# A two-layer streaming encoder: memory norm from four pair loads, GLU and all key blocks as three fp32r products, and a new order for the first stage

## Chip, core and metric

One core of one Trainium2 chip. The metric is the device time of one execution, in microseconds (us), as the median of several runs. TensorE multiplies matrices into PSUM banks; VectorE and ScalarE work on SBUF and PSUM tiles; GpSimd works on SBUF tiles; SyncE (SP) issues nearly all DMA loads from one queue, in order.

## The reference

512 frames of 1024 features run through two layers, each followed by cross-attention into 256 memory tokens.

```
mem_n = rms_norm(mem, mem_norm_g)
# layer 0
z = rms_norm(x) @ w_in                  # u_a, gate_a, val_b, glu_b, gate_b
y   = S5 scan of u_a (32 groups, complex states) + d * u_a
z   = gelu(y);  out = z * sigmoid(z @ glu_w + glu_b)
y_a = out * silu(gate_a)
c   = causal conv, width 31, of val_b * sigmoid(glu_b)
y_b = silu(layer_norm(c)) * silu(gate_b)
x   = x + concat(y_a, y_b) @ w_out
# layer 1: chunked attention, 16 heads, gated
# after each layer, 4 heads:
q, g = rms_norm(x) @ w_qg;  k, v = mem_n @ w_kv
x    = x + (softmax(q k^T / 16) v * silu(g)) @ w_o
```

All tensors are f32, and the final norm follows.

## The kernel before

Activations are kept with features on partitions: eight tiles of 128 features by 512 frames. A product of two f32 matrices is made of three products in fp32r: each operand is split into a high part (a rounding cast, ScalarE) and a low part (a subtraction, on GpSimd or VectorE), and TensorE adds high*high, high*low and low*high in one PSUM bank. `weights` (L172) loads a weight block into one of three `raw` buffers, casts it into one of two `whi` buffers and writes the rest into one of three `wlo` buffers; `proj` (L195) runs the 24 matmuls of a block in the order of sixteen with the high weights, then eight with the low ones. A few products are native f32: `whole` (L181) loads a block and TensorE multiplies it as it is. These are the GLU's four blocks (L917 to L922) and the key blocks 0, 1 and 2 of layer 0 (`NATIVE`, L659); the profile shows a native matmul as two records.

The first stage, up to about 262 us, is one list of jobs, `PLAN` (L700), in order of emission: `u` S5 inputs, `z` and `c` the convolution's gate and value (projections), `g` the eight gate projections, `v` a fourth of a convolution block (two of its eight weight tiles, 320 KB each, in `cw` buffers, L809), `t` the S5 tables, `a` the preparation of a scan (L528), `b` the scan of one of four slices (L550: TensorE, then some 11 us of VectorE), `o` its output (L599: TensorE, then a way through DRAM that changes the layout), `m` and `n` the sums and the scale of the memory norm, `l` and `s` the mean and the scale of the LayerNorm. Behind the list stand the gelu of the four S5 outputs (`zs`), `mem_norm` (L626), the GLU, the LayerNorm's application and the key and value blocks in `KVORDER`; then the output projection (`residual`, L946).

Emission order is not yet the order on the engines. A planner takes the recorded instructions, with its own costs for each, and draws up an order per engine before the run: by priority, which is the order of emission except in `tc.high_priority()`, by when inputs should be ready, and by when a buffer of the tile's tag is free (a tag has `bufs` slots). Inside `T.ordered` or `pinned` the order of emission is kept. On the chip each engine then runs its list in order and waits where it must. So matmuls of a projection and of a convolution block alternate in the trace.

`mem_norm` scales the memory by a broadcast in PSUM (`bcast`, L212, tag `acc`, one bank that the mean of the LayerNorm and all row sums use too). It loads eight tiles of 128 KB through two `mt` buffers; in layer 0 it also keeps unsplit copies in `uu` for the native keys. In layer 1 it runs beside the five last blocks of the attention's output projection (L1372).

At the start `first_c` and `third` (L777 to L782) are three projections in the three `proj` banks; the row scale `rb0` is broadcast behind the third, and the next projection needs a bank that `z0` (L792) has read.

## Time and profile before

| | |
|---|---|
| median of 3 runs | 997.92 us (994.61 to 998.61) |
| the profiled execution | 994.67 us |
| its span, first to last instruction | 992.9 us |
| TensorE busy | 956.0 us, 96% |
| weight loads of TensorE | 817.4 us, 82% |
| VectorE, ScalarE, GpSimd busy | 57%, 47%, 45% |
| mean granted TensorE clock | 0.991 |

How to read it: a busy TensorE record ends where the last result leaves, so the pace of a run of matmuls is read from the start of one group to the start of the next. The idle time before an instruction is followed by what ended it.

### The profile page before, as it was taken

To read this page: it belongs to the slowest core of one execution; us is meant where nothing else is said; L and a number is where in the kernel's file an instruction comes from. 1 tells how busy PE (TensorE), PEld (TensorE's weight loads), DVE (VectorE), ACT (ScalarE), POOL (GpSimd) and SP (SyncE) were. 2 spreads that over 40 slices of the span, in tenths; PEclk is the share of its full clock that TensorE was granted. 3 is DMA by queue.
4 is the path that set the end of the run, shared out by engine and by line. 5 is a ranking of instruction groups with operands and counts; after the bars stand their busy time and mean duration, and the time that the engine had idled before them with its cause. 6 is when DMAs were issued, how large, how long until landed. Compare 5 with 4: busy or idle time off the path is not lost.

```text
span 992.9 us, 14232 instructions
## 1 busy us (share of the span) xinstructions
PE 956.0 (96%) x5336; PEld 817.4 (82%) x5336; DVE 565.7 (57%) x1260; ACT 469.2 (47%) x845; POOL 442.3 (45%) x245
## 2 busy tenths in 40 slices
PE   9999999989999999999999999999999999999996
PEld 7788889759888888888787887878878998888895
DVE  7975257874344333452668767787667313333476
ACT  6333445565443434444456655656535543434352
POOL 1022333049676334457444435344327983443241
PEclk9999999999999999999999999999999999999998
DMA  8365656347523222223122222222214453222153
GB/s 290 119 191 180 195 157 191 104 159 229 162 98 91 79 81 69 64 96 107 64 75 75 75 68 92 75 75 75 64 43 138 151 189 107 64 85 76 52 169 107
DMA packets 53621, 113.71 MB, mean 115 GB/s; under 512 B 13233, under 2 KB 24625, under 8 KB 53553
## 3 DMA queue, kind: packets, MB, share of 16 engines
q1 hardware_dynamic: 53408, 112.74, 35.5%
q8 instruction: 42, 0.69, 0.3%
q14 instruction: 27, 0.21, 0.1%
q10 hardware_dynamic: 144, 0.07, 0.0%
HBM read 106.50 MB, written 6.29 MB: 114 GB/s over the span
## 4 chain that ended last, share of the span: by engine, by line
PE 34%; DVE 9%; issue 3%; ACT 2%; DMA 1%; POOL 1%; POOLq 0%; ACTq 0%; DVEq 0%
PE ps_proj L81 27%; PE ps_att L81 2%; PE ps_tr L84 2%; PE ps_acc L81 2%; PE ps_tr L81 1%; DVE pe L162 1%; ACT whi L168 1%; DVE ps_att L1270 1%; DVE tz L162 1%; DVE o L153 1%; DVE h L157 1%; POOL wlo L153 1%; ACT pe L1257 1%; DVE s L1269 1%; DMA mt<-in_memT_dram 1%
## 5 line engine op out<-in xcount | busy, mean ns | idle before, releaser
L153 POOL TENSOR_TENSOR wlo<-raw,whi 128x1024 fp32r<-128x1024 f32 x130 | 317.7, 2448 | 411.1 <-ACT whi L168 366.0
L81 PE MATMUL ps_proj<-h,whi 128*128 128x512 f32 x1184 | 299.4, 397 | 2.4 <-DVE ang L153 2.4
L81 PEld LDWEIGHTS ps_proj<-h,whi 128*128 128x128 f32 x1184 | 217.5, 188 | 47.4 <-issue 5.1
L168 ACT CAST whi<-raw 128x1024 fp32r<-128x1024 f32 x148 | 155.1, 1049 | 191.3 <-PE ps_proj L81 91.8
L81 PE MATMUL ps_proj<-h,wlo 128*128 128x512 f32 x592 | 151.7, 394 | 0.0
L81 PE MATMUL ps_proj<-og,whi 128*128 128x512 f32 (+1 forms) x672 | 135.0, 348 | 0.5 <-DVE og L153 0.5
L81 PEld LDWEIGHTS ps_proj<-h,wlo 128*128 128x128 f32 x592 | 111.0, 189 | 22.7
L81 PEld LDWEIGHTS ps_proj<-og,whi 128*128 128x128 f32 x672 | 107.6, 188 | 17.9 <-DVE og L153 2.0
L81 PE MATMUL ps_proj<-og,wlo 128*128 128x512 f32 (+1 forms) x344 | 73.4, 348 | 0.1
L81 PEld LDWEIGHTS ps_proj<-og,wlo 128*128 128x128 f32 x344 | 56.1, 188 | 8.9 <-POOL wlo L153 0.4
L153 DVE TENSOR_TENSOR pt<-ps_tr,pt 128x512 fp32r<-128x512 f32 (+1 forms) x80 | 39.9, 526 | 32.4 <-ACT pt L168 32.3
L168 ACT CAST pt<-ps_tr 128x512 fp32r<-128x512 f32 (+1 forms) x80 | 34.3, 460 | 49.1 <-PE ps_tr L84 48.8
L162 DVE TENSOR_SCALAR pe<-pe,s 128x256 f32<-128x256 f32 (+3 forms) x96 | 51.2, 555 | 1.4
L1257 ACT ACTIVATE pe<-ps_att,s 128x128 f32<-128x128 f32 (+3 forms) x64 | 33.6, 526 | 36.4 <-DVE s L162 32.5
L153 DVE TENSOR_TENSOR z<-ps_proj,rb 128x512 f32<-128x512 f32 x32 | 22.0, 688 | 46.3 <-PE ps_proj L81 46.2
L153 POOL TENSOR_TENSOR sa<-sa,sq 128x512 f32<-128x512 f32 (+1 forms) x28 | 38.9, 1388 | 18.9 <-ACT sq L228 18.2
L153 DVE TENSOR_TENSOR x<-ps_proj,x 128x512 f32<-128x512 f32 (+1 forms) x38 | 22.9, 603 | 41.7 <-PE ps_proj L81 41.7
L153 DVE TENSOR_TENSOR kv<-ps_proj,kv 128x256 fp32r<-128x256 f32 (+1 forms) x24 | 12.2, 511 | 60.2 <-ACT kv L168 59.3
L157 DVE SCALAR_TENSOR_TENSOR h<-x,par,h 128x512 fp32r<-128x512 f32 x24 | 38.6, 1613 | 13.5 <-ACT h L247 13.5
L84 PE MATMUL ps_tr<-ident,pe 128*128 128x128 f32 x224 | 35.9, 279 | 9.5 <-DVE pe L162 5.0
L81 PEld LDWEIGHTS ps_proj<-x,cw 128*128 128x128 f32 x320 | 39.1, 191 | 5.1 <-DMA cw<-in_cw_dram 3.1
L84 PEld LDWEIGHTS ps_tr<-ident,pe 128*128 128x128 f32 x224 | 27.1, 142 | 18.7 <-DVE pe L162 6.7
(244 smaller groups left out, 1448.3 us busy)
## 6 DMA issues: line engine op xcount, KB each, us to landing
raw<-in_xa_qg_dram SPq DMA_DIRECT2D x32, 512.0 KB, 3.4
...
```

Source lines behind the costliest of these rows:

```text
L81: return self.keep(nc.tensor.matmul(*args, **kw))
L84: return self.keep(nc.tensor.transpose(*args))
L153: (eng or V).tensor_tensor(out, a, b, op=op)
L157: V.scalar_tensor_tensor(out=out, in0=a, scalar=s, in1=b, op0=op0, op1=op1)
L162: V.tensor_scalar(out=out, in0=in0, scalar1=s1, scalar2=None, op0=op0)
L168: A.copy(hi, src)
L1257: A.activation(st_["pe"][i], ps[:, c:c + n], AF.Exp, bias=nb, accum_out=st_["sums"][:, i:i + 1])
L1269: V.reduce_max(init, ps[:, :nf], axis=AX.X)
L1270: V.tensor_tensor_reduce(out=ps[:, nf:n], in0=ps[:, nf:n], in1=st["tz"][:, MEM - (n - nf):], scale=1.0, scalar=init, op0=ALU.add, op1=ALU. ...
```

## The change

`mem_norm` takes four loads of two tiles each, all ahead of the broadcast, into `x` tiles in layer 0 and `kv` tiles in layer 1, and makes only the split form. The GLU's input is split, and its four blocks and all key blocks run as three products; `whole` is gone. Key and value weights of layer 0 have their low parts made on VectorE and GpSimd in turns (before: GpSimd), the GLU's on VectorE. Four key blocks come ahead of the LayerNorm's scale and of the GLU; `KVORDER` holds the rest. In `PLAN` `z0 c0` go ahead of `u0 u1`, `a1` ahead of `g2`, `b1` ahead of `z3 c3`, `a2` ahead of `g3`, `b2` ahead of `v2`, and `g4` to `g7` stand behind `b3`. The broadcast of `rb0` is put between the high and the low products of `third`. `cw` has three buffers instead of two, `s16` 28 instead of 48; the gated outputs are written over the gates.

```diff
--- before.py
+++ after.py
@@ -178,11 +178,6 @@
             split(raw, hi, lo, eng)
         return hi, lo
 
-    def whole(src, kt=8, n=P):
-        raw = tl("raw", (P, kt, n))
-        nc.sync.dma_start(raw, src)
-        return raw
-
     def mm3(ps, terms, cuts=()):
         prods = []
         for lo, hi in zip((0,) + tuple(cuts), tuple(cuts) + (len(terms),)):
@@ -256,7 +251,7 @@
             xs.append(t)
         return xs
 
-    l0p = Phase("l0", {"gate": 8, "uu": 8, "ev": 4, "cw": 2}).open()
+    l0p = Phase("l0", {"gate": 8, "uu": 8, "ev": 4, "cw": 3}).open()
 
     def norm_split(gname, goff=0):
         st = Stats()
@@ -623,28 +618,24 @@
             st.add(t, pin=True)
         return st
 
-    def mem_norm(rs, tag, raw_tag=None):
-        mm, raw = [], []
+    def mem_norm(rs, tag, load_tag):
+        mm = []
         with tc.high_priority():
+            ts_ = []
+            for i in range(0, KT, 2):
+                t = tl(load_tag, (P, 2, MEM))
+                nc.sync.dma_start(t, memT_d[i:i + 2].rearrange("i p s -> p i s"))
+                ts_ += [t[:, 0], t[:, 1]]
             rbm = bcast(rs, MEM)
-            for i in range(KT):
-                t = tl("mt", (P, MEM))
-                nc.sync.dma_start(t, memT_d[i])
+            for i, t in enumerate(ts_):
                 tt(t, rbm, t, ALU.mult)
                 e = rl(tag, (P, 2, MEM))
-                if raw_tag is None:
-                    mm.append(gsplit(t, pc("mem_g", i), e[:, 0], e[:, 1]))
-                else:
-                    if i % 2 == 0:
-                        m = tl(raw_tag, (P, 2, MEM))
-                    raw.append(m[:, i % 2])
-                    A.activation(raw[i], t, AF.Copy, scale=pc("mem_g", i))
-                    mm.append(split(raw[i], e[:, 0], e[:, 1], V))
-        return mm, raw
-
-    def token_major(outs, act, ws_d, eng=None):
+                mm.append(gsplit(t, pc("mem_g", i), e[:, 0], e[:, 1]))
+        return mm
+
+    def token_major(outs, act, ws_d, eng):
         for e in range(2):
-            wh, wl = weights(ws_d[e], kt=4, n=MEM, eng=eng)
+            wh, wl = weights(ws_d[e], kt=4, n=MEM, eng=eng())
             for low in range(2):
                 for t, o in enumerate(outs):
                     ts_ = slice(t * P, (t + 1) * P)
@@ -654,15 +645,15 @@
                             T.matmul(o, a[:, ts_], b[:, k, :], start=(e == 0 and low == 0 and t % 2 == 0 and k == 0 and j == 0),
                                      stop=(e == 1 and low == 1 and t % 2 == 1 and k == 3))
 
-    def kv_units(layer, mm, raw=None, native=()):
+    def kv_units(layer, mm, engs=(None,)):
+        count = [0]
+
+        def eng():
+            count[0] += 1
+            return engs[count[0] % len(engs)]
+
         def keys(i):
-            if ("k", i) in native:
-                w = whole(xa_k_d[layer, i])
-                ps = psum("proj")
-                for j in range(KT):
-                    T.matmul(ps[:, :MEM], w[:, j, :], raw[j], start=(j == 0), stop=(j == KT - 1))
-            else:
-                ps = proj(weights(xa_k_d[layer, i]), mm, n=MEM)
+            ps = proj(weights(xa_k_d[layer, i], eng=eng()), mm, n=MEM)
             e = rl("kv", (P, 2, MEM))
             with tc.high_priority():
                 split(ps[:, :MEM], e[:, 0], e[:, 1], V)
@@ -671,15 +662,7 @@
         def values(h):
             hi, lo = rl("kv", (P, 2, MEM)), rl("kv", (P, 2, MEM))
             ps = psum("proj")
-            if ("v", h) in native:
-                for e in range(2):
-                    w = whole(xa_v_d[layer, h, e], kt=4, n=MEM)
-                    for t in range(2):
-                        for j in range(4):
-                            T.matmul(ps[:, t * MEM:(t + 1) * MEM], raw[4 * e + j][:, t * P:(t + 1) * P], w[:, j, :],
-                                     start=(e == 0 and t == 0 and j == 0), stop=(e == 1 and t == 1 and j == 3))
-            else:
-                token_major([ps[:, :MEM], ps[:, MEM:]], mm, [xa_v_d[layer, h, e] for e in range(2)])
+            token_major([ps[:, :MEM], ps[:, MEM:]], mm, [xa_v_d[layer, h, e] for e in range(2)], eng)
             with tc.high_priority():
                 split(ps.rearrange("p (m c) -> p m c", m=2), hi, lo, V)
             vv[h] = (hi, lo)
@@ -695,12 +678,11 @@
             run["v"](i)
         return kv
 
-    KVORDER = [('k', 2), ('k', 0), ('k', 1), ('v', 3), ('k', 4), ('v', 0), ('k', 6), ('k', 3), ('k', 5), ('v', 2), ('v', 1), ('k', 7)]
-    NATIVE = [('k', 0), ('k', 1), ('k', 2)]
-    PLAN = "u0 u1 z0 c0 u2 u3 z1 c1 g0 v0 t0 g1 v0 v0 v0 a0 z2 b0 c2 v1 v1 v1 v1 g2 o0 a1 z3 b1 c3 v2 v2 v2 v2 g3 o1 a2 m0 g4 b2 v3 v3 v3 v3 g5 o2 a3 b3 n0 g6 l0 s0 o3 g7"
+    KVORDER = [('k', 4), ('v', 0), ('k', 5), ('v', 1), ('k', 6), ('v', 2), ('k', 7), ('v', 3)]
+    PLAN = "z0 c0 u0 u1 u2 u3 z1 c1 g0 v0 t0 g1 v0 v0 v0 a0 z2 b0 c2 v1 v1 v1 v1 a1 g2 o0 b1 z3 c3 a2 g3 o1 b2 v2 v2 v2 v2 a3 m0 v3 v3 v3 v3 o2 b3 g4 n0 g5 l0 g6 o3 g7"
     UENG = 'VVVVVVVVVVGG'
     GATE_V = (0, 3, 5, 7)
-    s5p = Phase("s5", {"l1": 2, "cs": 2, "m": 6, "g": 2, "y": 2, "s16": 48, "s32": 4}, side="right").open()
+    s5p = Phase("s5", {"l1": 2, "cs": 2, "m": 6, "g": 2, "y": 2, "s16": 28, "s32": 4}, side="right").open()
     l0cm = tc.tile_pool(name="l0s", bufs=1, side="right", reuse_waits="tile")
     l0 = l0cm.__enter__()
 
@@ -777,9 +759,14 @@
     first_c = [proj(weights(w_in_d[n], eng=V), h0) for n in (12, 8)]
     with tc.high_priority():
         rs0 = st0.done()
-    third = proj(weights(w_in_d[2], eng=V), h0)
-    with tc.high_priority():
-        rb0 = rb_tile(rs0)
+    third = psum("proj")
+    wh, wl = weights(w_in_d[2], eng=V)
+    for i, (a, b) in enumerate([(wh, 0), (wh, 1), (wl, 0)]):
+        for k in range(KT):
+            T.matmul(third, a[:, k, :], h0[k][b], start=(i == 0 and k == 0), stop=(i == 2 and k == KT - 1))
+        if i == 1:
+            with tc.high_priority():
+                rb0 = rb_tile(rs0)
     T.ordered = False
     tb = {}
 
@@ -886,11 +873,11 @@
             stt(conv[i], mu, -1.0 / 512, conv[i], ALU.mult, ALU.add)
             lst.add(conv[i], V)
 
-    def ln_scale(_):
+    def ln_scale():
         lst.rs = lst.done(1.0 / 512)
 
     stages = {"u": state_input, "z": conv_gate, "c": conv_input, "a": prep, "b": scan, "o": out, "g": gate, "m": mem_sums, "n": mem_scale, "v": conv_taps,
-              "l": ln_centre, "s": ln_scale, "t": tables}
+              "t": tables, "l": ln_centre}
     for job in PLAN.split():
         stages[job[0]](int(job[1:]))
     mrs = mem["rs"]
@@ -900,7 +887,7 @@
         t = tl("uu")
         stt(t, uP[sl].rearrange("p s j -> p (s j)"), pc("s5_d", sl), ys[sl].rearrange("p s j -> p (s j)"), ALU.mult, ALU.add)
         A.activation(t, t, AF.Gelu_apprx_tanh)
-        zs.append(t)
+        zs.append((t, split(t, rl("ev"), rl("uu"), V)))
 
     l0cm.__exit__(None, None, None)
     s5p.close()
@@ -909,33 +896,33 @@
     for i in range(8):
         if gates[i] is None:
             gate(i)
-    mm, mraw = mem_norm(mrs, "og", "uu")
+    mm = mem_norm(mrs, "og", "x")
+    run, kv0 = kv_units(0, mm, (G, V))
+    for i in range(4):
+        run["k"](i)
+    ln_scale()
 
     for g in gates:
         A.activation(g, g, AF.Silu)
     yg = [None] * 8
     for i in range(4):
-        w = whole(glu_w_d[i], 4)
-        ps = psum("proj")
-        for k in range(4):
-            T.matmul(ps, w[:, k, :], zs[k], start=(k == 0), stop=(k == 3))
-        sg = tl("ev")
+        ps = proj(weights(glu_w_d[i], kt=4, eng=V), [z[1] for z in zs])
+        sg = tl("sq")
         A.activation(sg, ps, AF.Sigmoid, bias=pc("glu_b", i))
-        tt(sg, zs[i], sg, ALU.mult, G)
-        o = tl("ev")
+        tt(sg, zs[i][0], sg, ALU.mult, G)
+        o = gates[i]
         tt(o.rearrange("p (j s) -> p j s", s=4), sg.rearrange("p (s j) -> p j s", s=4),
-           gates[i].rearrange("p (j s) -> p j s", s=4), ALU.mult)
+           o.rearrange("p (j s) -> p j s", s=4), ALU.mult)
         yg[i] = split(o, rl("og"), rl("og"))
 
-    run, kv0 = kv_units(0, mm, mraw, NATIVE)
     def ln_apply():
         lb = bcast(lst.rs, SEQ)
         for i in range(4):
             t = tt(conv[i], lb, conv[i], ALU.mult)
             A.activation(t, t, AF.Silu, scale=pc("ln_g", i), bias=pc("ln_b", i))
-            o = tl("ev")
+            o = gates[4 + i]
             tt(o.rearrange("p (j s) -> p j s", s=CP), t.rearrange("p (s j) -> p j s", s=CP),
-               gates[4 + i].rearrange("p (j s) -> p j s", s=CP), ALU.mult)
+               o.rearrange("p (j s) -> p j s", s=CP), ALU.mult)
             yg[4 + i] = split(o, rl("og"), rl("og"), V)
 
     ln_apply()
@@ -1369,7 +1356,7 @@
 
     kvp = Phase("kv1", {"kv": 16}, side="right").open()
     xap = Phase("xa1", XA).open()
-    mm, _ = mem_norm(mrs, "q")
+    mm = mem_norm(mrs, "q", "kv")
     residual(od_out_d, og, first=PARTS)
     h, st = norm_split("xa_g", 8)
     kv1 = kv_proj(1, mm)
```

## Rows read from the trace of the kernel before

**Rows 1.** The page of the whole span: busy time of each engine with its share of the span and instructions; and, from the costliest groups, the cast of a weight block (line, engine, operation, output<-inputs, shapes, count | busy us, mean ns of one | idle before, releaser).

```profile
PE 956.0 (96%) x5336; PEld 817.4 (82%) x5336; DVE 565.7 (57%) x1260; ACT 469.2 (47%) x845; POOL 442.3 (45%) x245
...
L168 ACT CAST whi<-raw 128x1024 fp32r<-128x1024 f32 x148 | 155.1, 1049 | 191.3 <-PE ps_proj L81 91.8
```

**Rows 2.** Busy time of the engines in the stretch from 192 to 262 us, from the GLU to the first block of the output projection. Columns: stretch, its length, busy us and instructions of each engine, granted TensorE clock, DMA share, GB/s.

```profile
192.00:262.00 70.00, 64.99 (x409) 53.58 (x408) 37.11 (x58) 41.01 (x64) 47.10 (x22) 1.00 0.57 182
```

**Rows 3.** TensorE's timeline, 32 to 45 us. Columns: start in us, length in us, engine, line, operation, output<-inputs, how many; in brackets the idle time before it and what ended it.

```profile
31.99 3.93 PE L81 MATMUL ps_proj<-h,whi 128*128 128x512 f32 x16
35.76 1.98 PE L81 MATMUL ps_proj<-h,wlo 128*128 128x512 f32 x8
37.58 1.02 PE L81 MATMUL ps_acc<-dg,ones 128*128 128x512 f32 x2
40.96 3.92 PE L81 MATMUL ps_proj<-h,whi 128*128 128x512 f32 x16 [2.36 <-DVE ang L153]
```

**Rows 4.** VectorE's timeline, 34 to 41 us.

```profile
34.65 0.87 DVE L162 TENSOR_SCALAR dg<-ident,s 128x128 f32<-128x128 f32 x4
...
37.20 1.22 DVE L153 TENSOR_TENSOR wlo<-raw,whi 128x1024 fp32r<-128x1024 f32 x1
...
39.27 1.02 DVE L153 TENSOR_TENSOR uu<-ps_att,rb 128x512 f32<-128x512 f32 x1
40.14 0.68 DVE L153 TENSOR_TENSOR ev<-ps_proj,rb 128x512 f32<-128x512 f32 x1
```

**Rows 5.** TensorE's timeline, the two holes of the middle of the first stage.

```profile
101.12 1.32 PE L81 MATMUL ps_proj<-x,cw 128*128 128x64 f32 x10 [1.62 <-DMA cw<-in_cw_dram]
...
155.59 1.30 PE L81 MATMUL ps_proj<-x,cw 128*128 128x64 f32 x10 [0.66 <-DVE m L153]
```

**Rows 6.** TensorE's timeline, the first and the last weight tiles of the first convolution block (`v0`).

```profile
62.85 2.33 PE L81 MATMUL ps_proj<-x,cw 128*128 128x64 f32 x20
...
83.91 1.22 PE L81 MATMUL ps_proj<-x,cw 128*128 128x64 f32 x10
```

**Rows 7.** The view of the convolution weight tiles: time from issue to landing of their 32 loads.

```profile
DMA to landing us min/median/max: 2.6/3.6/6.0
```

**Rows 8.** TensorE's timeline, 188 to 272 us.

```profile
188.98 1.09 PE L81 MATMUL ps_acc<-sa,ones 128*128 128x512 f32 x2
...
192.43 5.31 PE L81 MATMUL ps_proj<-uu,raw 128*128 128x512 f32 x12
197.58 0.95 PE L81 MATMUL ps_acc<-ones,sa 128*128 128x1 f32 x8
...
199.33 0.59 PE L81 MATMUL ps_acc<-dg,ones 128*128 128x256 f32 x2
...
205.37 5.40 PE L81 MATMUL ps_proj<-uu,raw 128*128 128x512 f32 x16 [1.15 <-ACT og L168]
212.55 3.72 PE L81 MATMUL ps_proj<-uu,raw 128*128 128x256 f32 x16 [1.79 <-ACT uu L641]
...
216.97 5.34 PE L81 MATMUL ps_proj<-uu,raw 128*128 128x256 f32 x24
...
226.30 1.20 PE L81 MATMUL ps_proj<-wlo,og 128*128 128x256 f32 x8 [1.38 <-POOL wlo L153]
...
242.01 1.98 PE L81 MATMUL ps_proj<-og,whi 128*128 128x256 f32 x16
243.82 1.07 PE L81 MATMUL ps_proj<-og,wlo 128*128 128x256 f32 x8
...
268.44 2.00 PE L81 MATMUL ps_proj<-og,whi 128*128 128x512 f32 x8
270.27 1.07 PE L81 MATMUL ps_proj<-og,wlo 128*128 128x512 f32 x4
```

**Rows 9.** VectorE's groups by form, 199 to 240 us: the gating of the LayerNorm branch's four tiles and of the GLU's four, and the scaling of the memory tiles. Columns as in rows 1.

```profile
L153 DVE TENSOR_TENSOR ev<-x,gate 128x512 f32<-128x512 f32 x4 | 9.9, 2505 | 0.8 <-ACT x L935 0.8
...
L153 DVE TENSOR_TENSOR ev<-ev,gate 128x512 f32<-128x512 f32 x4 | 5.2, 1298 | 1.0 <-POOL ev L153 0.9
L153 DVE TENSOR_TENSOR mt<-ps_acc,mt 128x256 f32<-128x256 f32 x8 | 3.2, 422 | 1.8 <-DMA mt<-in_memT_dram 1.2 <-PE ps_acc L81 0.4
```

**Rows 10.** VectorE's timeline, first and last work of the fourth scan (`b3`).

```profile
174.84 0.69 DVE L153 TENSOR_TENSOR m<-ps_att,cs 128x512 f32<-128x512 f32 x1 [4.97 <-PE ps_att L81]
...
184.70 1.28 DVE L153 TENSOR_TENSOR hh<-m,m 128x508 f32<-128x508 f32 x2
```

**Rows 11.** ScalarE's timeline, the copy of the last S5 output and the last gelu.

```profile
188.76 0.59 ACT L610 COPY y<-ps_att 128x512 f32<-128x512 f32 x1 [0.72 <-PE ps_att L81]
...
197.58 0.63 ACT L902 ACTIVATE uu<-uu 128x512 f32<-128x512 f32 x1 [1.15 <-DVE uu L157]
```

**Rows 12.** TensorE's timeline, second layer's attention.

```profile
484.52 0.30 PE L81 MATMUL ps_att<-qk,qk 128*128 128x128 f32 x1 [1.71 <-ACT qk L1160]
...
486.44 3.48 PE L81 MATMUL ps_proj<-h,wlo 128*128 128x512 f32 x8
```

**Rows 13.** Busy time by stretch, just behind those rows. Columns as in rows 2; the granted clock is a share of 2.4 GHz.

```profile
487.00:488.00 1.00, 1.00 (x3) 0.73 (x3) 0.15 (x1) 1.00 (x4) 0.14 (x1) 0.50 0.00 0
```

**Rows 14.** TensorE's timeline, the start of the second layer's key blocks.

```profile
771.06 2.08 PE L81 MATMUL ps_proj<-q,whi 128*128 128x256 f32 x16
...
776.56 1.22 PE L81 MATMUL ps_proj<-q,wlo 128*128 128x256 f32 x8 [0.55 <-POOL wlo L153]
```

## Prediction

> **What bounds the kernel now.** I read the page's busy shares first: TensorE is busy 96% of the span [rows 1], so a change counts only by what it does to TensorE's own work or to one of the few holes in it. Second, TensorE's timeline, where the bracket at a line's end is a hole and what ended it. From 270 us on the change touches almost nothing that TensorE does; before that the holes are a wait behind the first norm [rows 3], one for convolution weights and one for the scan [rows 5], and three at the end of the first stage, between the gated linear unit (GLU) and the first value blocks [rows 8]. Third, in that last stretch, the other engines: none of ScalarE, VectorE and GpSimd is full [rows 2], so those holes come from the order of the work, not from a full engine.
>
> **Part 1, three products instead of one native product.** GLU: sixteen native products of 512 columns, each two records. Twelve records, six products, start at 192.43 and the next work at 197.58 [rows 8]: 0.858 us each, 13.7 us. In the three-product form eight matmuls of 512 columns take from 268.44 to 270.27 [rows 8], 0.229 us each; 48 take 11.0. Saved: 2.7 us. Keys: 24 records, twelve native products of 256 columns, take 5.34 us, 0.445 each; three blocks have 24 products, 10.7 us. A three-product block runs sixteen matmuls from 242.01 to 243.82 [rows 8], 0.113 each, 24 in 2.7; three blocks 8.1. Saved: 2.6 us. Together 5.3 us of work that TensorE has no longer. The price lies elsewhere. ScalarE gets casts for three more key blocks at 1.05 [rows 1], four half-size ones for the GLU and four of its input, some 8 us. Of the layer's sixteen key and value weights half go to VectorE at 1.22 [rows 4], 9.8 us, and with the GLU's four and its input some 15. I put both at nothing, as ScalarE is busy 41 and VectorE 37 of 70 us there [rows 2]; if the cover goes, it shows as a wait for a weight split, of which the largest there now is 1.38 us [rows 8].
>
> **Part 2, the first norm's broadcast inside the third projection.** Its diagonal is written by 35.52 [rows 4]. The broadcast matmul starts at 37.58, behind the third projection's eight low products; the change puts it behind the sixteen high ones, at 35.76 [rows 3], 1.8 us sooner, and the copy to `rb` with it. The plan also puts `z0` ahead of `u0`: `z0` reads the projection bank that TensorE waits for, and now stands behind `u0`'s 1.02 us on VectorE, at 40.14 [rows 4]. What is late next is the weight split on VectorE, which ends at 38.42 [rows 4]; `z0` would be done at about 39.1, and TensorE, finished with the third projection at 38.6 as now, waits 0.5 us instead of 2.36 [rows 3]. Gain 1.8, bounds 0 and 2.36; I take 1.7.
>
> **Part 3, three buffers for convolution weights.** One wait of 1.62 us ends with such a load [rows 5]. A third slot starts each load one tile earlier; I take 1.3, between 0 and 1.62. The 0.66 us before 155.59 [rows 5] ends with the scan; 0.4 for it, between 0 and 0.66. The smaller rings for the tables I put at nothing: their operations follow each other on VectorE, and the table is long done when the first scan needs it.
>
> **Part 4, the plan and the end of the first stage.** Three holes, 1.15, 1.79 and 1.38 us, 4.3 together [rows 8]. Why they are there: the memory's broadcast runs at 199.33, though the mean that occupies the same single bank was computed at 188.98; the normaliser's sums, which the program puts first, take the bank at 197.58 [rows 8]. So the eight memory tiles come late, and the key blocks meet them. In the change `ln_scale` goes behind four key blocks, so the broadcast follows the mean; and the four pair loads no longer wait for two small buffers to be read. Where do the scans go? The last scan holds VectorE from 174.84 to 185.98 [rows 10]. Behind it the old plan has `g6`, `o3`, `g7`; the new has `g4`, `g5`, `g6`, `o3`, `g7`, two projections of 24 times 0.229, 11.0 us, more. So the mean, which waits for that scan on VectorE, comes some 11 us sooner as TensorE counts, and the memory's broadcast with it: about 182 on the old clock, when TensorE reaches the keys at 192.4. Eight tiles at 0.42 for the scaling [rows 9] and, with GpSimd quiet, about as much for the low half need some 9 us: in time. The last output leaves TensorE at 188.76 and its gelu ends at 198.2 [rows 11], 9.5 us, and the new split adds 1.3; behind it now stand `g7`, 5.5 us, and four key blocks, 10.8. So the GLU finds its input ready. All 4.3 us could go; I leave 1.3 for key weights, which are split in turns on GpSimd and VectorE. Gain 3.0, from 4.3 to a loss worked out under the second rival.
>
> **Part 5, the second layer's memory norm.** Its loads move from `mt` into `kv` tiles, four instead of eight, ahead of five residual blocks on SP's queue. The keys start at 771.06 without a hole, right behind the residual [rows 14], so earlier memory tiles bring nothing. The 0.55 us before 776.56 ends with a weight split on GpSimd, which the change does not touch [rows 14]. If the new loads come late, VectorE, in order, stands with the last head's output behind it; the rows show no such wait, so I bound it by the longest hole of the early stage, 2.36, and by a gain of 0.55, and take 0.
>
> **Sum.** 5.3 + 1.7 + 1.3 + 0.4 + 3.0 = 11.7 us. The profiled execution took 994.67 us (span 992.9, 1.8 around it), so 983.0. It is the lower end of the runs shown; their median, 997.92, lies 3.25 above it, and I give the forecast on the median: 986.2 us.
>
> **Rivals.**
>
> First, *only the work goes*: the order on each engine is drawn up by a planner before the run, so what I say of the plan need not come out, and holes of the same size may open elsewhere, as they did at 101.12 and 155.59 [rows 5]. Then 5.3 us remain: 997.92 - 5.3 = 992.6. For it: the holes have different causes, so no one remedy takes them all. Against it: each has one in the change that I can follow. Chance 0.16.
>
> Second, *the memory tiles are late all the same*. VectorE's two-input operations here are slow beside a busy GpSimd: the gating of a tile took 1.30 us for the GLU's four and 2.51 us for the four behind them, when weight splits ran on GpSimd without a break [rows 9]. Every second key block has its weights split on GpSimd, just then. At 0.42 plus 2 us for a tile, eight need 19.4 us instead of 9; broadcast at 182, they end at 201.4, when the first key block should end at 195.1: TensorE stands some 6 us, and the new splits behind it on VectorE cost 2 or 3 more. Net gain 11.7 + 1.3 - 9 = 4.0: 993.9. The Trainium skill, page GPSIMD Engine Reference, section 8 (Key points), says that GpSimd shares its memory interfaces with VectorE and that operations with two inputs there contend. By that rule this rival would hold whenever GpSimd splits a block. The trace agrees on the slowing [rows 9]. Against it: with half the splits on VectorE, GpSimd is no longer busy without a break. Chance 0.12.
>
> Third, *slower: the convolution weights become the pace*. The new plan puts `v2` four times and `v3` four times with only `a3` and `m0` between: sixteen weight tiles. Each is about 1.1 us of TensorE (two in 2.33, with the last one's end); now eight of them are spread from 62.85 to 85.1 [rows 6], with projections between. Three slots give a tile every third of landing plus 1.1 us: 1.57 at the median landing of 3.6, 2.37 at the longest of 6.0 [rows 7]. Sixteen tiles then lack 7.5 to 20.3 us, unless the planner moves `g4` and `g5` in between. If it does not, the time is slower by half a per cent once more than 16.7 us are lost, at landings of 5.3 us and up; at 5.7 it is 18.7, giving 997.92 - 11.7 + 18.7 = 1004.9. It would be dearer still if TensorE's clock fell: after the hole of 1.71 us at 484.52 the clock was granted at 0.50, which is 1.2 GHz, and eight matmuls took 3.48 us [rows 12, 13] instead of 1.98 [rows 3]. The Trainium skill, page TensorE: Matmul & The Clock Gate, Part 1, says the same of an engine that has idled; behind the holes of the early stage it stayed at 1.00 [rows 2], so the sum has none. Against the rival: TensorE does interleave projections with these tiles now. Chance 0.08.
>
> Fourth, *everything goes*: 5.3 + 2.4 + 1.6 + 0.7 + 4.3 + 0.55 = 14.9 us: 983.1. Chance 0.1.
>
> **How the numbers follow.** The forecast, with its bounds on parts 2 to 5, covers 983.5 to 990 and has 0.54. The range takes in the fourth rival, counted from the profiled execution instead of the median (994.67 - 14.9 = 979.8), and the first two: 980 to 995. Outside are the third rival and tails of the rest, 0.16. About 0.5%, 5.0 us, is what a measurement here can tell from no change. Faster by more: forecast, fourth rival and half of the first (it lies on the edge), 0.72. Within: the other half and the second, 0.2. Slower: the third, 0.08.
>
> **What would show it.** Right: GLU and key blocks as runs of sixteen and eight; a hole of under 1 us in place of the one at 40.96; the memory's broadcast on TensorE ahead of the normaliser's sums; key blocks with no hole ahead of the GLU; the output projection starting some 11 us sooner. Wrong: a hole before the first key block ended by a memory tile (second rival), convolution tiles at 1.6 us and more apart with nothing between (third), holes of 4 to 6 us in new places (first). Were the sum right at the output projection and wrong at the end, the loss would lie in the second layer's memory norm or in the planner's order behind it.

## The result, and the profile after

The changed kernel takes 1011.54 us (median of four runs, 1008.03 to 1015.16), the kernel before beside it 997.79: ratio 1.015, 95% interval 1.0114 to 1.0185. The forecast was 986.2 us, 11.7 less than before; it is 13.75 more. The profiled execution took 1009.22 us.

First, the page: the span, and the busy time of the engines with share and instructions (answers to [rows 1]).

```profile
span 1007.4 us, 14325 instructions
PE 964.3 (96%) x5376; PEld 831.5 (83%) x5376; DVE 589.8 (59%) x1276; ACT 473.5 (47%) x848; POOL 433.3 (43%) x240
```

TensorE is busy for 8.3 us longer, though it has less to do. So the lost time is not only in holes: matmuls take longer.

Second, where. TensorE's timeline at the start of the output projection, which had begun at 261.59 (the kernel before) and has the same work behind it in both:

```profile
275.44 1.99 PE L81 MATMUL ps_proj<-og,whi 128*128 128x512 f32 x8
277.27 1.08 PE L81 MATMUL ps_proj<-og,wlo 128*128 128x512 f32 x4
```

13.85 us later. From there to the end it is 732.0 us here and 731.3 before: by these two profiles everything was lost in the first stage.

Third, TensorE's timeline there; the bracket is the idle time ahead of the line and what ended it. From 37 to 62 us (answers to [rows 3]):

```profile
37.83 3.94 PE L81 MATMUL ps_proj<-h,whi 128*128 128x512 f32 x16 [0.47 <-DVE ev L153]
...
51.51 5.51 PE L81 MATMUL ps_proj<-h,whi 128*128 128x512 f32 x16 [2.48 <-DVE uu L153]
56.86 2.01 PE L81 MATMUL ps_proj<-h,wlo 128*128 128x512 f32 x8
58.70 3.79 PE L81 MATMUL ps_proj<-h,whi 128*128 128x512 f32 x16
```

The hole of 2.36 us is 0.47, as forecast, and another of 2.48 stands two projections behind it. The sixteen matmuls behind that one take 5.51 us, the next sixteen 3.79.

From 130 to 168 us (answers to [rows 5, 6]):

```profile
132.19 1.97 PE L84 MATMUL ps_tr<-ident,w 128*128 128x128 f32 x8 [3.19 <-DVE w L153]
...
149.50 1.32 PE L81 MATMUL ps_proj<-x,cw 128*128 128x64 f32 x10 [0.43 <-DMA cw<-in_cw_dram]
152.11 2.39 PE L81 MATMUL ps_proj<-x,cw 128*128 128x64 f32 x10 [1.28 <-DMA cw<-in_cw_dram]
...
157.81 2.23 PE L81 MATMUL ps_proj<-x,cw 128*128 128x64 f32 x10
...
165.66 1.22 PE L81 MATMUL ps_proj<-x,cw 128*128 128x64 f32 x10
```

The transposes of the third scan's preparation wait 3.19 us for VectorE; the convolution's tiles wait for their loads, and then each takes 2.2 to 2.4 us instead of 1.2 until 165.

From 200 us to the output projection (answers to [rows 8]):

```profile
200.16 0.59 PE L81 MATMUL ps_acc<-dg,ones 128*128 128x256 f32 x2
...
205.40 0.95 PE L81 MATMUL ps_acc<-ones,sa 128*128 128x1 f32 x8
209.79 2.04 PE L81 MATMUL ps_acc<-dg,ones 128*128 128x512 f32 x2 [3.44 <-DVE dg L162]
...
213.04 5.14 PE L81 MATMUL ps_proj<-og,whi 128*128 128x256 f32 x28 [0.78 <-DVE og L157]
...
235.81 1.07 PE L81 MATMUL ps_proj<-ev,wlo 128*128 128x512 f32 x4
236.72 2.05 PE L81 MATMUL ps_proj<-og,whi 128*128 128x256 f32 x16
...
242.42 1.21 PE L81 MATMUL ps_proj<-wlo,og 128*128 128x256 f32 x8 [0.89 <-POOL wlo L153]
245.45 2.10 PE L81 MATMUL ps_proj<-whi,og 128*128 128x256 f32 x16 [1.83 <-ACT whi L168]
248.77 1.19 PE L81 MATMUL ps_proj<-wlo,og 128*128 128x256 f32 x8 [1.22 <-DVE wlo L153]
```

The memory's broadcast runs at 200.16, where it was, not at 182. What held it and the tiles behind it (VectorE, TensorE and ScalarE of the changed kernel):

```profile
187.79 0.48 DVE L162 TENSOR_SCALAR dg<-ident,s 128x128 f32<-128x128 f32 x2
...
193.77 1.10 PE L81 MATMUL ps_acc<-sa,ones 128*128 128x512 f32 x2
...
194.91 1.89 DVE L157 SCALAR_TENSOR_TENSOR x<-ps_acc,x 128x512 f32<-128x512 f32 x3 [1.28 <-PE ps_acc L81]
...
199.04 0.68 DVE L157 SCALAR_TENSOR_TENSOR x<-ps_acc,x 128x512 f32<-128x512 f32 x1
...
212.03 2.91 ACT L242 ACTIVATE og<-x,par 128x256 fp32r<-128x256 f32 x7 [4.67 <-DVE uu L157]
```

Its diagonal was written by 188.27, but the single bank went to the LayerNorm's mean first, at 193.77. VectorE, with a weight split, a gate and sums between its four centring steps, read that bank until 199.72. Seven of the eight memory tiles then stood on ScalarE until VectorE had used the last S5 output (212.03).

Ahead of the first key block stands the LayerNorm's whole chain (205.40, 209.79), planned there although the program puts it behind four key blocks. The GLU runs from 225.80 to 236.72, 10.9 us for 48 matmuls: that saving came out as worked out. Behind it the value weights are late.

Fourth, the granted clock, where it was not 1.00: busy time by stretch (columns as in [rows 2]; behind the instruction counts the clock, DMA share and GB/s).

```profile
54.00:56.00 2.00, 2.00 (x6) 1.60 (x5) 2.00 (x4) 0.00 (x0) 0.00 (x0) 0.50 0.76 258
...
134.00:136.00 2.00, 2.00 (x6) 1.61 (x6) 0.00 (x0) 0.59 (x1) 0.00 (x0) 0.50 0.49 191
...
158.00:160.00 2.00, 2.00 (x12) 2.00 (x11) 0.00 (x0) 0.00 (x0) 0.00 (x0) 0.50 0.49 164
...
214.00:216.00 2.00, 2.00 (x12) 2.00 (x11) 2.00 (x6) 1.98 (x4) 0.00 (x0) 0.50 0.59 195
```

Behind the holes at 51, 132, 152 and 209 us TensorE ran at 1.2 GHz, to about 56, 138, 165 and 216 us. In the profiled execution of before there is one such stretch ahead of the output projection, from 8.7 to 12.1 us, and none from 30 us on:

```profile
10.00:12.00 2.00, 2.00 (x6) 1.58 (x5) 1.98 (x4) 1.89 (x3) 0.00 (x0) 0.50 1.06 416
```

**The account.** For every kernel I took three numbers from its profiled execution, up to the start of the output projection: the holes of TensorE over 0.3 us from 30 us on, summed; the clock's price from 30 us on, TensorE's busy time in stretches of 2 us times (1 - granted clock); and that start itself. Before has 9.47 us of holes, no price, and 261.59, so 252.1 us (261.59 - 9.47) are left. Less the work saved (5.3, or 2.6 with key blocks alone), plus holes, plus clock, is "by the sum". The work saved is the forecast's own term, so the column tests it too. Ratios are to the kernel before, timed beside each.

| kernel | ratio, 95% interval | holes | clock | by the sum | start |
|---|---|---|---|---|---|
| before | 1 | 9.5 | 0 | - | 261.6 |
| changed | 1.015 [1.0114, 1.0185] | 16.5 | 14.3 | 277.6 | 275.4 |
| E1 | 1.0094 [1.0057, 1.0131] | 20.8 | 10.3 | 277.9 | 275.6 |
| E2 | 1.014 [1.0102, 1.0178] | 14.2 | 12.9 | 279.2 | 277.3 |
| E3 | 1.0154 [1.0097, 1.0211] | 15.4 | 11.7 | 273.9 | 273.7 |
| E4 | 1.0096 [1.0062, 1.0129] | 19.4 | 12.9 | 279.1 | 277.3 |
| E5 | 1.012 [1.0065, 1.0175] | 15.6 | 13.6 | 276.0 | 275.4 |
| E6 | 1.0042 [1.0014, 1.007] | 17.1 | 6.3 | 270.2 | 270.1 |
| E7 | 0.9972 [0.9943, 1.0] | 9.4 | 3.4 | 264.9 | 261.2 |
| E8 | 1.0009 [0.9986, 1.0032] | 10.4 | 6.4 | 268.9 | 267.6 |
| E9 | 1.0037 [1.0013, 1.006] | 15.5 | 6.6 | 268.9 | 269.4 |
| E10 | 1.0092 [1.0061, 1.0122] | 14.3 | 6.2 | 270.0 | 269.7 |
| E15 | 1.0047 [1.0022, 1.0073] | 15.3 | 3.8 | 265.9 | 266.5 |
| E16 | 1.0046 [1.0024, 1.0067] | 14.7 | 5.7 | 267.2 | 267.7 |
| E17 | 1.0098 [1.0066, 1.0129] | 20.7 | 5.4 | 272.9 | 272.0 |
| E18 | 0.9992 [0.9972, 1.0012] | 12.5 | 6.0 | 265.3 | 265.6 |
| E21 | 1.0144 [1.011, 1.0179] | 21.0 | 9.3 | 277.1 | 275.8 |
| E22 | 1.0015 [0.9992, 1.0038] | 10.5 | 5.8 | 265.8 | 265.3 |
| E23 | 1.0082 [1.0047, 1.0117] | 16.6 | 5.7 | 269.1 | 269.2 |
| E24 | 0.9975 [0.9952, 0.9998] | 9.1 | 2.2 | 260.8 | 259.9 |

The sum meets the start within 2.4 us in all but E7 (3.7). The stretch of before at 8.7 to 12.1 us, a price of 1.6 us, is in the 252.1 and has no counterpart in the others: their first projection starts at 17.99 to 19.17 us, that of before at 20.30. With it taken off every sum is 1.6 lower, and all meet the start within 2.2 us, E7 too. For the changed kernel: 5.3 us of work saved, 7.0 more of holes, 14.3 of clock, less 1.6, is 14.4 against 13.85 measured. A profile is one execution, and the times of one kernel lie some 12 us apart (before: 990.51 to 1002.92), so ratios decide; the profiles of E10, E15, E16, E21, E23 and E24 are each of the fastest run of their kernel.

### The profile page after: what moved, and what is told of

The parts are those of the page before. It is cut to its first block, busy times and chain, and to the rows that moved or that the text cites. A ratio compares the mean times of both kernels' runs of the same rounds, so it can differ in the third digit from the quotient of the medians.

```text
span 1007.4 us, 14325 instructions
## 1 busy us (share of the span) xinstructions
PE 964.3 (96%) x5376; PEld 831.5 (83%) x5376; DVE 589.8 (59%) x1276; ACT 473.5 (47%) x848; POOL 433.3 (43%) x240
## 4 chain that ended last, share of the span: by engine, by line
PE 35%; DVE 9%; issue 3%; ACT 2%; POOL 1%; DMA 1%; POOLq 0%; ACTq 0%; DVEq 0%
PE ps_proj L81 28%; PE ps_att L81 2%; PE ps_tr L84 2%; PE ps_acc L81 2%; PE ps_tr L81 1%; DVE pe L162 1%; DVE o L153 1%; DVE ps_att L1257 1%; DVE tz L162 1%; POOL wlo L153 1%; DVE q L157 1%; ACT whi L168 1%; DVE s L1256 1%; POOL sa L153 0%; DVE qk L153 0%
## 5 line engine op out<-in xcount | busy, mean ns | idle before, releaser
L153 POOL TENSOR_TENSOR wlo<-raw,whi 128x1024 fp32r<-128x1024 f32 x125 | 302.4, 2421 | 453.9 <-ACT whi L168 387.5
L81 PEld LDWEIGHTS ps_proj<-h,whi 128*128 128x128 f32 x1184 | 220.0, 190 | 49.1 <-issue 4.5
L168 ACT CAST whi<-raw 128x1024 fp32r<-128x1024 f32 (+1 forms) x155 | 160.7, 1038 | 187.7 <-PE ps_proj L81 106.9
L81 PE MATMUL ps_proj<-og,whi 128*128 128x512 f32 (+1 forms) x720 | 143.9, 347 | 1.2 <-DVE og L157 0.8
L81 PEld LDWEIGHTS ps_proj<-og,whi 128*128 128x128 f32 x720 | 115.8, 191 | 19.8 <-DVE og L153 1.6
L81 PE MATMUL ps_proj<-og,wlo 128*128 128x512 f32 (+1 forms) x368 | 76.8, 344 | 0.5 <-POOL wlo L153 0.5
L81 PEld LDWEIGHTS ps_proj<-og,wlo 128*128 128x128 f32 x368 | 59.2, 188 | 9.3 <-POOL wlo L153 0.9
L153 DVE TENSOR_TENSOR wlo<-raw,whi 128x1024 fp32r<-128x1024 f32 (+1 forms) x30 | 37.8, 1259 | 25.7 <-ACT whi L168 25.4
L153 POOL TENSOR_TENSOR sa<-sa,sq 128x512 f32<-128x512 f32 (+1 forms) x28 | 41.0, 1465 | 15.9 <-ACT sq L223 15.3
L81 PEld LDWEIGHTS ps_proj<-x,cw 128*128 128x128 f32 x320 | 42.9, 209 | 3.3 <-DMA cw<-in_cw_dram 2.4
L81 PE MATMUL ps_proj<-x,cw 128*128 128x64 f32 (+4 forms) x320 | 42.9, 289 | 1.7 <-DMA cw<-in_cw_dram 1.7
```

Source lines behind the costliest of these rows:

```text
L81: return self.keep(nc.tensor.matmul(*args, **kw))
L153: (eng or V).tensor_tensor(out, a, b, op=op)
L168: A.copy(hi, src)
```

## The experiments

My theory was that the loss is in the order of the work: holes that the new order opens, and the clock behind them. The rivals: the splits as work on other engines; the convolution's loads; a dearer TensorE.

**E1 and E2: plan and products apart.** E1 is the changed kernel with the old plan (without `s0`, which the new code has elsewhere), E2 the kernel before with the new plan.

```diff
 E1:
-    PLAN = "z0 c0 u0 u1 ... a2 g3 o1 b2 v2 v2 v2 v2 a3 m0 v3 v3 v3 v3 o2 b3 g4 n0 g5 l0 g6 o3 g7"
+    PLAN = "u0 u1 z0 c0 ... g3 o1 a2 m0 g4 b2 v3 v3 v3 v3 g5 o2 a3 b3 n0 g6 l0 o3 g7"
 E2: the same the other way round in the kernel before, with s0 behind l0
```

> The changed kernel with the order of jobs of the kernel before (only s0 left out, as the LayerNorm scale stays behind four key blocks). Theory of the order: the loss comes from the new plan, which puts TensorE's scan work and convolution tiles where their inputs are not ready, and from the clock granted at 0.50 behind each such hole (2.5, 3.2 and 1.7 us of holes and some 12 us of clock before 170 us). Then this run has none of that, keeps the 5.3 us of saved work, and takes 990 to 998 us, at a mean clock of 0.985 or more. Theory of the splits: the loss comes from the added weight splits and the late memory tiles at the end of the stage; then it takes 1005 to 1012 us.

> The kernel before with the new order of jobs alone (s0 kept, behind l0). Theory of the order: the new holes and the fallen clock come with it, 1003 to 1012 us. Theory of the splits: 993 to 1000 us, as all the added work is absent.

E1 took 1004.15 us, E2 1008.54. Each part alone loses: 0.9 and 1.4%, the first near what the theory of the splits says, the second as that of the order says; neither holds alone. E1 has all of the change but the plan, not the products only. The two losses, 9.4 and 13.8 us, add up to more than the change's 13.75, so they overlap. In E2, TensorE's timeline shows the changed kernel's wait ahead of the third scan's transposes:

```profile
136.57 1.97 PE L84 MATMUL ps_tr<-ident,w 128*128 128x128 f32 x8 [3.22 <-DVE w L153]
```

E1 has holes in other places, ahead of the first key block (9.5 us from 195 to 206) and behind the GLU (3.96 and 2.59).

**E3 and E5: the memory tiles in another ring.** In the changed kernel the memory tiles are split into `og`, which lies over the scan's memory. E3 splits them into `h`; E5 also takes the GLU's sigmoid tiles from `h` instead of the two `sq` buffers.

```diff
-    mm = mem_norm(mrs, "og", "x")
+    mm = mem_norm(mrs, "h", "x")
-        sg = tl("sq")
+        sg = tl("h")      # E5
```

> The changed kernel with the split memory tiles of layer 0 in h tiles, not in og tiles. Theory of the place: the og tiles lie where the scan's tiles lay, so seven of eight memory tiles wait for the last S5 output to come back from DRAM (212 us), and the key blocks with them; in h they wait only for the last gate projection. The holes of 3.4 and 0.8 us at 210 us and the half clock behind them (3.4 us) shrink: 1002 to 1006 us by this kernel's profile of 1009, 3 to 7 us less. Otherwise, if the wait comes from the order on VectorE alone: no change, within 2 us.

> The changed kernel with the split memory tiles and the GLU's sigmoid tiles in h tiles (16 buffers) in place of og and of sq (2 buffers). Theory of the ring: with two sq buffers the third sigmoid waits for the first gating, and ScalarE, in order, stands with the casts of the value weights behind it (holes of 4.0 and 2.5 us at 239 to 245 us with the memory tiles in h alone, and 5 us of half clock). Those go: 6 to 12 us less than with the memory tiles alone in h, 996 to 1003 us. If the casts stand behind the gating for another reason: within 3 us of 1008.

1008.21 and 1010.92 us: no gain that can be measured. In E3 the holes at 209.79 and 213.04 became one of 1.30, and those behind the GLU grew to 3.96 and 2.49; in E5 these stayed, so the two buffers are not their cause.

**E4: the third scan's preparation and the taps spread.**

```diff
-    ... c3 a2 g3 o1 b2 v2 v2 v2 v2 a3 m0 v3 v3 v3 v3 o2 b3 g4 n0 g5 l0 g6 o3 g7
+    ... c3 g3 a2 o1 b2 v2 v2 g4 v2 v2 a3 m0 v3 v3 g5 v3 v3 o2 b3 n0 l0 g6 o3 g7
```

> The changed kernel with three moves in the plan: a2 behind g3, g4 and g5 in the middle of v2 and of v3. Theory of the order: the hole of 3.2 us that waits for a2 and the two for convolution weights (1.7 us) go, with the half clock behind them (some 10 us): 6 to 14 us less than the changed kernel, 996 to 1004 us. Theory of the splits: within 3 us of the changed kernel.

1003.79 us, by the ratio 0.5% below the changed kernel, with intervals that overlap. The transposes' hole is gone, but loads still end one of 1.46 at 159, and the key blocks wait 4.65 and 1.96 us, having fewer projections in front: the holes moved.

**E6: old plan and other rings together.** E1 with both edits of E5.

> The same two moves with the old order of jobs. Theory of the ring and of the place: the six holes from 195 to 248 us (16 us) and 10 us of half clock of the old order with three products shrink to a few us, and the 5.3 us of saved work show: 983 to 992 us, faster than the kernel before. If the splits themselves are too much for ScalarE and VectorE: 1000 us and more.

1002.66 us, 0.4% over before and 0.5% under E1, with intervals that overlap; the 983 to 992 of the theory did not come. The largest holes left, at the end of the stage, TensorE's timeline:

```profile
191.85 1.10 PE L81 MATMUL ps_acc<-sa,ones 128*128 128x512 f32 x2 [2.11 <-DVE s L157]
195.99 1.22 PE L81 MATMUL ps_acc<-dg,ones 128*128 128x256 f32 x2 [3.04 <-DVE x L157]
...
235.34 3.42 PE L81 MATMUL ps_proj<-whi,h 128*128 128x256 f32 x16 [3.95 <-ACT whi L168]
241.60 2.08 PE L81 MATMUL ps_proj<-wlo,h 128*128 128x256 f32 x8 [2.84 <-DVE wlo L153]
```

What holds up the casts behind the GLU: VectorE's and ScalarE's timelines in E6.

```profile
227.79 3.19 DVE L153 TENSOR_TENSOR gate<-h,gate 128x512 f32<-128x512 f32 x1 [2.43 <-POOL h L153]
```

```profile
231.01 0.62 ACT L168 CAST og<-gate 128x512 fp32r<-128x512 f32 x1 [5.22 <-DVE gate L153]
...
234.25 1.03 ACT L168 CAST whi<-raw 128x1024 fp32r<-128x1024 f32 x1
```

ScalarE stands 5.22 us in front of the GLU's gated tile, in order, and the weight casts behind it are late; the tile waits for VectorE, VectorE for GpSimd's product. The changed kernel has the same wait: 5.18 us ahead of the cast at 243.26.

**E7 and E8: two parts alone in the kernel before.** E7 has the third `cw` buffer (and the smaller ring that makes room), E8 the broadcast inside the third projection and `z0` first.

```diff
 E7:
-    "ev": 4, "cw": 2})        ... "s16": 48
+    "ev": 4, "cw": 3})        ... "s16": 28
 E8: third as in the change; PLAN = "z0 c0 u0 u1 u2 u3 ..." and the rest as before
```

> The kernel before with three cw buffers and 28 small table slots, nothing else: the third part of the prediction by itself. By the prediction: the hole of 1.62 us at 101 us goes, 1 to 2 us less than before. Theory of the order (any change of buffers makes the planner draw up another order, with holes elsewhere and the clock fallen behind them): anything up to 8 us more.

> The kernel before with the broadcast of rb0 inside the third projection and z0 c0 ahead of u0 u1, nothing else: the second part of the prediction by itself. By the prediction: 1.7 us less than before. Theory of VectorE as the bound from 20 to 60 us (it is busy there without a break, by 10-us stretches): the hole of 2.36 us at 41 us shrinks and one of about the same size opens at 51 us, where the next projection waits for a bank that u2 reads; with the half clock behind it, 0 to 3 us more than before.

E7 took 994.46 us beside 997.63; the hole at 101 stayed with three slots:

```profile
101.78 1.32 PE L81 MATMUL ps_proj<-x,cw 128*128 128x64 f32 x10 [1.68 <-DMA cw<-in_cw_dram]
```

E8 took 999.2, no difference: the hole of 2.36 became 0.48, and at 51 us stands the one of the changed kernel, with slow matmuls behind it:

```profile
51.27 5.29 PE L81 MATMUL ps_proj<-h,whi 128*128 128x512 f32 x16 [2.51 <-DVE uu L153]
```

**E9, E15, E16, E10: the end of the stage with the old plan.** All start from E6. E9 frees the chain found there; E15 adds to it the LayerNorm's centring out of the way; E16 to that the gated tiles' low half on VectorE; E10 is E6 with native products for the GLU.

```diff
 E9:
-        tt(sg, zs[i][0], sg, ALU.mult, G)
+        tt(sg, zs[i][0], sg, ALU.mult, V)
 E15: E9, l0 out of PLAN, and ln_centre(0) ahead of ln_scale(), behind four key blocks
 E16: E15, and
-        yg[i] = split(o, rl("og"), rl("og"))
+        yg[i] = split(o, rl("og"), rl("og"), V)
 E10: E6, and
-        ps = proj(weights(glu_w_d[i], kt=4, eng=V), [z[1] for z in zs])
+        w = ... # raw load
+            T.matmul(ps, w[:, k, :], zs[k][0], start=(k == 0), stop=(k == 3))
```

> The kernel with the old plan, three products and the memory and sigmoid tiles in the h ring, with one edit more: the product sigmoid times z of the GLU runs on VectorE instead of GpSimd. In that kernel VectorE's gate product at 227.79 waited 2.43 us for GpSimd's sigmoid product, ScalarE's cast of the gated tile at 231.01 waited 5.22 us for VectorE's gate, and the casts of key and value weights stood behind it in ScalarE's list; TensorE then had holes of 3.95 us (ended by a weight cast on ScalarE) and 2.84 us (ended by a weight split on VectorE), with a stretch at a granted clock of 0.50 behind them. Theory: the price of the splits is this order of casts; with the GpSimd step out of the chain the two holes shrink to under 2 us together and the clock stays up there, 5 to 9 us less than 1002.7: 993.5 to 997.5. Rival: VectorE, which takes the product over, is then the late one, the holes return ended by it, and the time stays within 2 us of 1002.7.

> As the kernel with the sigmoid product on VectorE, and the centring of the convolution's LayerNorm moved from its place in the plan (behind g6) to behind the four key blocks, so that nothing of that norm lies between the last scan and the memory's norm on VectorE, in the single bank or on TensorE. Theory: the holes of 2.11, 3.04 and 1.06 us at 192 to 198 us, which VectorE's s, x and ScalarE's h ended, go down to 3 us together, and the clock stays up behind them: 4 to 8 us less than that kernel, near 990. Rival: the memory norm's own chain (mean, root, broadcast, eight tiles) is the late one whatever stands between; one hole of 5 us or more remains before the first key block, and the time moves by less than 2 us.

> As the kernel before it, and the low half of the GLU's gated tiles is formed on VectorE instead of GpSimd, so that GpSimd has nothing of the gating. Theory of contention: VectorE's permuted gate product took 3.19 us beside a busy GpSimd and 1.05 us without it; with four splits fewer on GpSimd, weight splits meet less of it and the time falls by 1 to 3 us more. Rival: VectorE has four operations more (0.67 us each) ahead of its weight splits and TensorE waits for these: 1 to 3 us more.

> The kernel with the old plan, three products and the memory and sigmoid tiles in the h ring, with the GLU back to native products (no split of its input and its weights); all key blocks stay three products. It parts the change's first part into its halves. Theory: the GLU's splits cost nothing by themselves and its saving is the 2.7 us of TensorE work, so the time is 2 to 4 us above 1002.7. Rival: the eight casts and eight subtractions of the GLU are what pushes the key and value weights late; without them the holes at 235 and 242 us shrink by more than 3 us and the time is 1 to 4 us below 1002.7.

E9 took 1000.52 us: the two holes went from 6.8 to 3.0 together, so the chain was their cause; but the ratios of E6 and E9 hardly differ, so the time does not show what the chain costs. E15 took 1001.02 and its rival held: the three holes ahead of the first key block, 6.2 us, became 4.55 and 1.06, and the time did not move. What is late is the memory norm's own chain:

```profile
193.94 1.19 PE L81 MATMUL ps_acc<-dg,ones 128*128 128x256 f32 x2 [4.55 <-DVE dg L162]
```

E16, 999.82, is no different. E10 took 1005.02, above E6 (1.0092 against 1.0042, intervals that overlap) as the theory has it; yet its holes behind the GLU, up to 241 us, are 4.0 us together, from 6.8. So the GLU's casts have a part in the late weights, but taking them back gains no time here.

**E17, E18, E21, E22: the key blocks behind the GLU again.** By now the kernels with the old plan and three products stood 5.6 to 9.5 us ahead of the first key block (E3 and E5, with the new plan and the memory tiles in `h`, only 1.3). The change puts four key blocks in front of the GLU; before, the GLU's products ran while the memory tiles were made.

```diff
-    for i in range(4):
-        run["k"](i)        # ahead of the GLU
...
+    for i in range(4):
+        run["k"](i)        # behind the GLU, ahead of ln_apply()
 E17: E9 with it; E18: E15 with it, ln_centre(0) and ln_scale() staying ahead of the GLU;
 E21: the changed kernel with it; E22: E17 with native products for the GLU
```

> The kernel with the old plan, three products, the memory tiles in h and the sigmoid product on VectorE, with the first four key blocks moved from ahead of the GLU to behind it. Theory: the GLU's 48 matmuls, 11 us, then stand beside the memory norm's chain as they did in the kernel before; the holes of 2.11, 3.04 and 1.06 us at 194 to 201 us shrink to 2.5 us together or less and the clock stays up: 6 to 9 us less than 1000.5, 991 to 995, and below the kernel before. Rival: the GLU's input (gelu of the last output, cast and low half) is later than the memory tiles, and a hole of 4 us or more opens ahead of the GLU instead: 998 or more.

> As the kernel with the key blocks behind the GLU, and the LayerNorm's centring taken out of the plan and put behind the memory norm. Theory: the memory tiles are no longer what TensorE waits for, so it makes little difference: within 2 us of that kernel. Rival: VectorE's four centring operations and sums still stand ahead of the GLU's input; taking them back saves 2 to 4 us more.

> The changed kernel itself with one edit: the first four key blocks stand behind the GLU. Theory: of its holes those of 3.44 and 0.78 us at 209.79 and 213.04, ahead of and in the first key block, go, with their stretch at 0.50 (208 to 217, some 4 us); the ones at 51, 132, 152 and 242 to 252 stay: 5 to 8 us less than 1011.5, 1003 to 1006. Rival: the late memory tiles, which lie over the scan's memory, are later than the GLU's end too, or the holes open ahead of the GLU: within 2 us of 1011.5.

> As the kernel with the key blocks behind the GLU, with the GLU back to native products: the change's first part for the key blocks alone. Theory: 2.7 us more work than with three products for the GLU and the same holes: 2 to 4 us above that kernel. Rival: native products, which need no split of the input, start sooner and cover the memory norm for longer; the holes shrink by more than 2.7 us and it is no slower.

E17 took 1005.65 us: the rival. The low half of its GLU input came late: on VectorE it stands at 201.07, behind the LayerNorm's centring and the eight memory tiles (191.3 to 200.6 us):

```profile
201.81 1.22 PE L81 MATMUL ps_proj<-uu,whi 128*128 128x512 f32 x2 [5.64 <-DVE uu L153]
```

E18, with the centring behind the memory norm, forms the same input at 193.69, ahead of the memory tiles, and took 995.54 beside 996.26: level with the kernel before, and 10 us better than E17, where I had expected no more than 4. E22 took 997.81, better than E17: its rival held too, native products need no split of the input. E21 took 1009.73, as the changed kernel: in the new plan a hole of 7.79 us opened ahead of the GLU. So, with the old plan, the order of key blocks and GLU alone is not the cause, and the LayerNorm's place alone is not (E15 against E9); together they are: E18's interval lies below those of E9, E15 and E17. In the new plan only the first of the two was tried.

**E23 and E24: can the saved work be had?** E23 is E18 with the LayerNorm's centring behind the GLU and the GLU's matmuls pinned to program order (`T.ordered`); E24 is E18 with native products for the GLU, that is, the old plan with the change's key blocks in another place and without its GLU.

> As the kernel with the key blocks behind the GLU and the LayerNorm's centring behind the memory norm, with the centring put behind the GLU in the program and the GLU's matmuls pinned to program order. In that kernel TensorE waited 4.76 us at 201.21 for the LayerNorm's mean, which shares its bank with the memory's broadcast and had to wait for eight memory tiles on VectorE, and 1.13 us behind it for the GLU's input. Theory: with the mean out of the way that hole goes and the clock stays up: 3 to 6 us less than 995.5, 990 to 992.5, below the kernel before by half a per cent. Rival: the GLU's last input, whose first step stands behind the same eight tiles on VectorE, ends the hole instead; a hole of 3 us or more remains and the time stays within 2 us of 995.5.

> As that kernel, with native products for the GLU. Theory: 2.7 us more work on TensorE, but the hole of 4.76 us at 201 is a wait by the clock on the wall, and the longer native products stand in part of it: within 2 us of 995.5, so the GLU's saving is worth nothing here. Rival: work saved is time saved also here: 2 to 4 us above 995.5.

E23 took 1003.67, above both ranges: TensorE waits for the mean all the same (3.87 us), and new holes of 2.33 and 5.11 opened. E24 took 993.72 us beside 995.99, the one kernel whose whole interval lies below 1, by 0.0002: 0.25% under before, too little to build on from one of nineteen intervals. TensorE's timeline:

```profile
189.52 7.03 PE L81 MATMUL ps_proj<-uu,raw 128*128 128x512 f32 x16
196.38 1.02 PE L81 MATMUL ps_acc<-sa,ones 128*128 128x512 f32 x2
197.24 3.61 PE L81 MATMUL ps_proj<-uu,raw 128*128 128x512 f32 x8
201.94 2.81 PE L81 MATMUL ps_proj<-uu,raw 128*128 128x512 f32 x6 [1.09 <-ACT sq L223]
...
219.19 2.08 PE L81 MATMUL ps_proj<-h,wlo 128*128 128x256 f32 x8 [2.40 <-DVE wlo L153]
```

Where E18 waits 4.76 us for that mean at 201.21, the native products, two records each, start at once and fill the time. They also leave VectorE without the GLU's splits: the memory's broadcast comes 4.4 us behind the scan's last step there (184.11 to 188.55), in E18 6.7 (188.57 to 195.31). The GLU's 2.7 us of saved work is worth nothing that can be measured in this place.

## Why the prediction was wrong

**Two terms failed, by about as much: the holes, which were to fall by 6.4 us (1.7 + 1.3 + 0.4 + 3.0) and rose by 7.0, and the clock, put at nothing: "behind the holes of the early stage it stayed at 1.00 [rows 2], so the sum has none".** The clock costs up to 14.3 us in the changed kernel, more than all I forecast as gain. I read it from one execution of before; [rows 2] shows 192 to 262 us alone, and that execution has a stretch at 0.50 at 8.7 to 12.1 us. I priced a clock at 0.50 in the slower rival only. In the 18 experiments each profile has such a stretch between 30 us and the output projection. A hole should have been priced with what follows: behind the 1.28 us ahead of 152.11 came 13 us at 0.50, a price of some 6.5.

**Part 2, "I take 1.7".** "Waits 0.5 us instead of 2.36" came out, 0.47. The step that failed took this for a gain: VectorE has no slack there (the third column, busy in 29.88 of 30 us from 20 to 50, before and then changed), so the wait moved to 51 us. Alone (E8) the part is worth nothing that can be measured.

```profile
20.00:50.00 30.00, 27.64 (x125) 22.32 (x124) 29.88 (x160) 8.88 (x13) 0.00 (x0) 1.00 0.43 146
```

```profile
20.00:50.00 30.00, 28.46 (x125) 22.35 (x124) 29.88 (x161) 10.04 (x14) 0.00 (x0) 1.00 0.54 175
```

**Part 3, "I take 1.3" for the third slot.** The hole stayed with three slots (E7, 1.68 us). E7's 0.3% gain touches zero at the interval's end, and is not that hole's. In the changed kernel, with the new plan, it is gone, and holes of 0.43 and 1.28 us that end with such loads stand at 149.50 and 152.11.

**Part 4, "All 4.3 us could go".** The broadcast was to come at about 182 and came at 200.16. Counted in TensorE's work the mean did come sooner: 12.6 us of work lie between it (193.77) and the hole ahead of the first key block (206.35), before 3.4 us up to the GLU. The steps that failed are "and the memory's broadcast with it" and "some 9 us: in time". I counted how much TensorE work the plan puts behind the mean, and left out what VectorE has before the broadcast: it ran 6.4 us behind the mean, though its diagonal was ready 5.5 us ahead of it. The eight tiles then took until 216.4, 16.2 us, as their casts wait for the last S5 output; in E3, with the tiles in `h`, they take 9.7 us (197.76 to 207.42) and the hole there is 1.3. The planner also put the LayerNorm's chain between the broadcast and the key blocks. Above all I treated "behind four key blocks" as a gain only: the GLU had covered the memory norm's chain, and in front of it the key blocks have no cover (E15 against E18, with the old plan). The steps "the GLU finds its input ready" and 10.9 us for it were right.

**Part 1, "I put both at nothing".** The 5.3 us nearly came out: 10.9 us for the GLU, 2.82 for a key block instead of 2.7 (starts at 220.15, 222.97 and 225.80), and the account meets the measured starts with them. The price of the splits that the traces show is not their work: ScalarE and VectorE were not full. It is their place in ScalarE's list, behind a cast that waits 5.22 us (E6): the holes behind it fell from 6.8 to 3.0 us in E9, though the time did not. And saved work is worth what its place leaves of it: with native products for the GLU the time rose from E6 to E10 (intervals that overlap), fell from E17 to E22, and did not measurably move from E18 to E24.

**Part 5, 0:** right as far as the two profiles show: 732.0 against 731.3 us from the output projection to the end.

**The rivals.** The first, new holes in other places, named the mechanism but had them "of the same size" and ended faster. The third, slower by the convolution's loads and the clock, is seen at 149 to 165 us, 1.7 us of holes and some 6.7 of clock, but is one of four places. The second has one of them: memory tiles done late, though not for GpSimd's splits: GpSimd stands idle from 207.3 to 220.6 us. On contention, VectorE's gate took 3.19 us in E6 at 227.79, while GpSimd split a weight, and 1.06 at 234.23. The Trainium skill, page GPSIMD Engine Reference, section 8 (Key points), says that instructions of VectorE with two inputs in SBUF contend with GpSimd; the trace agrees. E16, which takes four splits from GpSimd, shows no gain from it.

**The clock by itself.** Executions of one kernel have the same order and different clocks. Over the 104 executions of before that were timed beside the experiments the mean granted clock goes from 0.981 to 0.996 and the time from 1002.92 to 990.51 us; a line through them falls by 8.5 us for each 0.01 of clock (correlation 0.94). The changed kernel's four executions have 0.968 to 0.977, median 0.9735, those of before 0.988: 0.0145 less, by that line an estimate of 12.3 of the 13.75 us. What else differs from one execution to the next, longer waits above all, is in that line too.

What stays open: which move of the plan costs what (E2 has them all, E4 takes back some), and why the clock falls behind one hole and not behind another.
